# Transformer-block kernel on one Trainium2 core: two of v's seven products computed chunk by chunk beside the first norm, all of x loaded ahead, two combinations kept unsplit in DRAM, and the memory tokens ordered behind two state-space chunks

## The chip, the cores and the metric

The kernel runs on one core of a Trainium2 chip, as one program with one launch. The metric is device time in microseconds (us). A core has five engines that run their own instruction queues side by side: TensorE (PE in the profile; its weight loads are PEld), VectorE (DVE), ScalarE (ACT), GpSimd (POOL) and SyncE (SP), from whose queue this kernel issues all its DMAs.

## The reference, cut to what matters

One layer of a hybrid decoder trunk on x of 1024 tokens by 1024 channels, float32. The change touches the beginning of the first sub-layer, and the place where the second sub-layer's memory tokens are prepared.

```python
h = rms_norm(x, g_pre_mix[l])
q, k, v, z, xbc, dt_raw, ga, gs = _split(h @ w_in[l], IN_SIZES)
o_att = stick_breaking_attention(q..., k..., v...)      # 16 heads of 64
o_ssm = ssd_branch(z, xbc, dt_raw, conv_w[l], conv_b[l], dt_bias[l], a_log[l], d_skip[l], g_ssm_norm[l])
merged = jax.nn.sigmoid(ga) * (o_att @ w_br_att[l]) + jax.nn.sigmoid(gs) * (o_ssm @ w_br_ssm[l])
x = x + rms_norm(merged @ w_mix_out[l], g_post_mix[l])
h = rms_norm(x, g_pre_xa[l])
mem_n = rms_norm(mem, g_mem[l])                         # 256 memory tokens
x = x + rms_norm(memory_cross_attention(h, mem_n, w_xq[l], w_xkv[l], w_xo[l]), g_post_xa[l])
h = rms_norm(x, g_pre_ffn[l])
x = x + rms_norm(swiglu(h, w_gu[l], w_down[l]), g_post_ffn[l])
```

`h @ w_in` is one product of 1024 x 1024 with 1024 x 10272; v has 1024 of its columns, z 2048, dt 32.

## The kernel before, in words

**Split operands.** A float32 operand is rounded to the matmul's type as a high half (`hi_sb`, L85, a copy on ACT or POOL), and the rest becomes a low half (`lo_of`, L96, a subtraction on VectorE or POOL). A product of two operands is three matmuls: high by high, high by low, low by high (`mm3`, L99; `acc3`, L226, for four blocks of the inner dimension).

**Seven products in place of eight.** h transposed is cut into quarters: b11 and b21 are the two channel halves of tokens 0 to 511, b12 and b22 those of tokens 512 to 1023. Winograd's form of the 2 x 2 block product needs b11, b21, b22 and the combinations t1 = b12 - b11, t2 = b22 - t1, t3 = b22 - b12, t4 = b21 - t2, and on the weights a11, a21, a22, a12 the sums s1 = a21 + a22, s2 = s1 - a11, s3 = a11 - a21, s4 = a12 - s2. The seven products are a11 by b11, s2 by t2, a12 by b21, s1 by t1, s3 by t3, s4 by b22 and a22 by t4.

**First stage (L283 to L366).** x is loaded in chunks of 128 tokens (`load_x`, L293; four buffers of `t4`, so chunks 2, 6, 3 and 7 are loaded only when a buffer comes free). `chunk_pair(c)` (L319) takes chunks c and c + 4: `normed` (L305) squares on ACT (L309), makes the reciprocal root on POOL (L167, L168) and scales on VectorE (L310); `turned` (L313) does eight transposes per chunk on TensorE into PSUM; then come the splits of b11, b21 and b22 (L327, L328), the combinations on VectorE (L339 to L344) and their splits, those of t1, t3, t4 and b12 with the low half on POOL. The halves of b12 go to DRAM (`hb_d`) for the attention's projections. dt is made here with 48 small matmuls per pair (L354).

**v and z (L367 to L466).** `token_major(j, c0, put, i0)` (L392) runs the seven products of one block of 1024 columns: j = 0 is v, j = 1 and 2 are z. `product` (L400) splits four weight blocks and issues 48 matmuls of 128 x 512. The weight blocks come from DRAM into the ten buffers of `rp` ("zraw", L269). For v the sums s1, s2, s3 are made on VectorE (L424 to L428), for z on POOL. Then come the x, B, C columns and gates in `pair` (L523), dt's chain (`dt_chain`, L540), the attention, and the state-space mixer.

**State-space stage (from L839).** `prep(n)` (L916) loads the rows of chunk n and makes its decays (L930 to L939); two chunks are prepared ahead. `memory(m)` (L1058) loads and normalises 128 memory tokens; their key and value projections are spread over the first chunks (`mem_quanta`, L1072).

**What sets the order.** Every engine runs its queue in order. The order in a queue is not that of the code: a planner lays the instructions out before the launch, from modelled durations (`schedule_with_timeline_sim=True`, L1710), and a tile takes a buffer of its pool when one comes free. `behind(marks)` (L219) orders what it encloses behind given instructions on the same engine. `FILL_LEFT` and `FILL_RIGHT` (L31) are unused bytes that fix where later tiles lie.

## Time and profile before

| | |
|---|---|
| median of 3 runs | 2610.64 us (2610.59 to 2611.89) |
| the profiled execution | 2612.0 us |
| its span, first to last instruction | 2610.3 us |
| granted TensorE clock, mean | 0.984 |
| TensorE busy in the span | 2501.3 us (96%) |
| VectorE, ACT, POOL busy | 1801.2, 1142.9, 877.7 us |

Times in the profile are microseconds from the span's start. In a timeline row stand the start, the busy time, the engine, the line of the kernel, the operation, what it writes and reads, and the count; in brackets the idle time before it and what ended that. In a grouped row stand busy time, mean ns of one, and the idle time before. A row of the table by stretches has the stretch, its length, the busy time of PE, PEld, DVE, ACT and POOL with the instructions counted, the granted TensorE clock as a share of full speed, the busy share of the DMA engines and GB/s.

### The profile page before, as it was taken

The page shows a single profiled execution, that of the slowest core. Times are in us where ns is not written, and L with a number is a line of the kernel's source. Part 1 is how long each engine was busy: PE and PEld are TensorE (multiplying, and loading weights), DVE is VectorE, ACT ScalarE, POOL GpSimd, SP SyncE. Part 2 cuts the span into 40 slices and gives each one's busy share as a digit, 9 for nine tenths or more (in the row PEclk, how much of TensorE's full clock was granted, in tenths as well). Part 3 has the DMA queues.
Part 4 walks back from the last instruction along what each step waited for, and adds up shares of the span by engine and source line. Part 5 has one row for each costly group of instructions (what it writes and reads, how often), then busy time and mean ns, then how long its engine had stood idle before and what let it go on. Part 6 is the DMA issues. An engine that isn't in the chain of part 4 may idle for free. (4 is left out here: it accounts for less than half of the span.)

```text
span 2610.3 us, 32705 instructions
## 1 busy us (share of the span) xinstructions
PE 2501.3 (96%) x12026; PEld 2074.0 (79%) x12026; DVE 1801.2 (69%) x2084; ACT 1142.9 (44%) x2037; POOL 877.7 (34%) x682
## 2 busy tenths in 40 slices
PE   5999999999999999989999999999999999999997
PEld 5888887788878878878888778887787888887886
DVE  7446778776587887588888665415459666666996
ACT  5333454555465665456544312314324333333342
POOL 5212544453211112235555150101114333324763
PEclk7999999999999999989999999999999999999999
DMA  5331343333534343355332472311232232323223
GB/s 175 113 106 57 123 135 95 107 114 115 149 96 108 99 116 97 92 174 191 110 92 70 146 248 82 123 55 49 86 116 72 78 93 73 97 73 153 97 112 130
DMA packets 250667, 288.51 MB, mean 111 GB/s; under 512 B 16767, under 2 KB 173064, under 8 KB 250122
## 3 DMA queue, kind: packets, MB, share of 16 engines
q1 hardware_dynamic: 250506, 286.41, 35.1%
q8 instruction: 95, 1.56, 0.2%
q14 instruction: 66, 0.54, 0.1%
HBM read 196.56 MB, written 73.01 MB: 103 GB/s over the span
## 5 line engine op out<-in xcount | busy, mean ns | idle before, releaser
L750 DVE TENSOR_TENSOR_SCAN n<-n,mask 128x128 f32<-128x128 f32 (+7 forms) x128 | 188.8, 1500 | 23.5 <-ACT n L749 22.2
L97 DVE TENSOR_TENSOR sw<-sf,sw 128x512 fp32r<-128x512 f32 x150 | 127.1, 859 | 67.6 <-ACT sw L94 67.2
L198 POOL TENSOR_TENSOR sf<-wr,wr 128x512 f32<-128x512 f32 x38 | 57.5, 1514 | 275.1 <-DMA wr<-in_w_gu_dram 123.0
L767 ACT ACTIVATE wth<-tr,mone 128x512 fp32r<-128x512 f32 x192 | 110.4, 584 | 82.3 <-PE tr L764 81.6
L94 ACT ACTIVATE sw<-sf 128x512 fp32r<-128x512 f32 x150 | 92.0, 626 | 111.4 <-PE mm L231 96.0
L768 DVE SCALAR_TENSOR_TENSOR wtl<-tr,wth 128x512 fp32r<-128x512 f32 x192 | 99.7, 543 | 49.7 <-ACT wth L767 49.7
L94 ACT ACTIVATE sw<-wr 128x512 fp32r<-128x512 f32 x113 | 71.0, 629 | 127.6 <-PE mm L231 127.5
L231 PE MATMUL mm<-h,sw 128*128 128x512 f32 x320 | 124.8, 391 | 1.8 <-DVE sw L97 1.8
L100 PE MATMUL mm<-oth,bw 128*128 128x512 f32 (+1 forms) x320 | 122.4, 383 | 3.5 <-DVE a L1048 2.4
L229 PE MATMUL mm<-h,sw 128*128 128x512 f32 x320 | 122.8, 392 | 2.9 <-ACT h L94 2.3
L230 PE MATMUL mm<-h,sw 128*128 128x512 f32 x320 | 125.2, 391 | 0.0
L97 DVE TENSOR_TENSOR sw<-wr,sw 128x512 fp32r<-128x512 f32 x113 | 102.9, 911 | 26.0 <-ACT sw L94 18.0
L102 PE MATMUL mm<-oth,bw 128*128 128x512 f32 (+1 forms) x320 | 119.7, 374 | 0.0
L101 PE MATMUL mm<-otl,bw 128*128 128x512 f32 (+1 forms) x320 | 119.1, 372 | 0.0
L97 DVE TENSOR_TENSOR zl<-zr,zh 128x512 fp32r<-128x512 f32 x84 | 67.6, 810 | 72.4 <-ACT zh L94 72.3
L509 DVE SCALAR_TENSOR_TENSOR b<-b,prmT,b 128x1023 f32<-128x1023 f32 (+2 forms) x72 | 107.6, 1494 | 13.7 <-ACT b L507 13.1
L90 POOL TENSOR_SCALAR v<-va 128x512 fp32r<-128x512 f32 x16 | 20.5, 1286 | 284.8 <-PE av L777 164.8
L167 POOL TENSOR_SCALAR rstd<-ms 128x1 f32<-128x1 f32 x82 | 32.5, 396 | 238.0 <-ACT x L1269 112.0
L749 ACT ACTIVATE n<-sc 128x512 f32<-128x512 f32 (+1 forms) x192 | 88.6, 493 | 45.7 <-PE tr L764 28.9
L94 ACT ACTIVATE zh<-zr 128x512 fp32r<-128x512 f32 x84 | 52.4, 630 | 114.0 <-PE mb L415 55.4
L100 PE MATMUL p<-bw,h 128*128 128x512 f32 x256 | 98.9, 391 | 3.3 <-DVE x L1271 2.4
L200 POOL TENSOR_TENSOR sf<-wr 128x512 f32<-128x512 f32 x38 | 62.7, 1650 | 111.8 <-DVE sw L97 111.8
(596 smaller groups left out, 8247.3 us busy)
## 6 DMA issues: line engine op xcount, KB each, us to landing
wr<-in_w_gu_dram SPq DMA_DIRECT2D x80, 256.0 KB
wr<-in_w_in_dram SPq DMA_DIRECT2D x36, 512.0 KB
zr<-in_w_in_dram SPq DMA_DIRECT2D x24, 512.0 KB
gu_d<-t SPq DMA_DIRECT2D x44, 256.0 KB
wraw<-in_w_in_dram SPq DMA_DIRECT2D x20, 512.0 KB
x<-in_x_dram SPq DMA_DIRECT2D x16, 512.0 KB
zs_d<-zo SPq DMA_DIRECT2D x32, 256.0 KB
xs_d<-b SPq DMA_DIRECT2D x32, 256.0 KB
```

The costliest lines, as they stand in the source:

```text
L94: A.activation(o, i, AF.Copy)
L97: eng.tensor_tensor(o, i, hi.bitcast(F32), ALU.subtract)
L100: first = T.matmul(ps, sh, mh, start=start, stop=False)
L101: T.matmul(ps, sh, ml, start=False, stop=False)
L102: T.matmul(ps, sl, mh, start=False, stop=stop)
L229: T.matmul(ps, w[0][:, k, :], b[0][:, k, :], start=first and k == 0, stop=False, skip_group_check=True)
L230: T.matmul(ps, w[0][:, k, :], b[1][:, k, :], start=False, stop=False, skip_group_check=True)
L231: T.matmul(ps, w[1][:, k, :], b[0][:, k, :], start=False, stop=last and k == 3, skip_group_check=True)
L509: V.scalar_tensor_tensor(acc[:, sh:], y[:, :S - sh], cw(3 - sh, f), acc[:, sh:], ALU.mult, ALU.add)
L750: V.tensor_tensor_scan(nt[:, 0:L][:, ::-1], nt[:, 0:L][:, ::-1], mask[:, S - L:][:, ::-1], 1.0, ALU.mult, ALU.max)
L767: A.activation(wh[:, t0 * P:], pt[:, t0 * P:], AF.Identity, bias=mone)
L768: V.scalar_tensor_tensor(wl[:, t0 * P:], pt[:, t0 * P:], -1.0, wh[:, t0 * P:].bitcast(F32), ALU.add, ALU.subtract)
```

## The change

x0 is loaded first, then the gain and the other chunks, four of the eight into weight buffers, so that no load waits for a buffer. v's a11 and a12 are loaded in between and split once (`wv`). After each chunk pair, `first_products` runs the products of b11 and b21 for the chunk before, 24 matmuls of 128 x 512, keeps the first sum in `uv` and stores the first part of v. b12, t3 and t4 are stored unsplit (`hb_d`, `tc_d`); t3 and t4 are loaded and split in `rest_of_v`, which runs v's other five products, t1 first, with a11 and a12 loaded a second time; b12 is split when the attention needs it. dt takes high and low weights in one operand of 64 columns, 40 matmuls per pair in place of 48, and the two parts are added in `dt_chain`. The parameter columns and small loads move behind the last x; ACT gets a Square of one column at the very start; the transposes have five PSUM buffers in place of six. In the state-space stage the memory tokens' loads and first ACT work are ordered behind the loads and exponentials of the second chunk. z runs as before, with its sums on POOL.

```diff
-FILL_LEFT, FILL_RIGHT = 128, 224
+FILL_LEFT, FILL_RIGHT = 96, 224
...
-    dt_d = scr("dt_d", [32, S])
-    hb_d = [scr(f"hb_d{i}", [P, 4, HALF]) for i in range(2)]
+
+    dt_d = scr("dt_d", [2, 32, S])
+    hb_d = scr("hb_d", [P, 4, HALF])
+    tc_d = [scr(f"tc_d{i}", [P, 4, HALF]) for i in range(2)]
...
+    warm = mk(cp, [P, 1], F32, "warm")
+    A.activation(warm, mone, AF.Square)
...
-            bt = pool(p1, "b12t", 4)
+            bt = pool(p1, "b12t", 3)
+            vh = pool(p1, "vsplit", 8)
             mp = pool(p1, "memp")
             mt4 = pool(p1, "t4mem", 2)
             psp = pool(p1, "ps1", 2, PSUM)
+            xts = {}
+
+            def load_x(c):
+
+                xts[c] = mk(t4, [P, D], F32, "x4") if c % 4 >= 2 else mk(rp, [P, 2, HALF], F32, "zr").rearrange("p a t -> p (a t)")
+                return nc.sync.dma_start(xts[c], x_in[c * P:(c + 1) * P, :])
+
+            load_x(0)
             gx = load_gain(mp, "g_pre_mix")
-            xts = {}
-
-            def load_x(c):
-                xts[c] = mk(t4, [P, D], F32, "x4")
-                nc.sync.dma_start(xts[c], x_in[c * P:(c + 1) * P, :])
-
-            for c in (0, 4, 1, 5):
+            for c in (4, 1, 5):
                 load_x(c)
             wd = mk(mp, [P, KT, 32], F32, "wd")
             nc.sync.dma_start(wd, colblock(w_in, C_DT, 32))
-            wdh, wdl = [mk(mp, [P, KT, 32], F32R, n) for n in ("wdh", "wdl")]
-            hi_sb(wdh, wd, "p")
-            lo_of(wdl, wd, wdh, G)
+            raws = [block(0, C_V)]
+            for c in (2, 6):
+                load_x(c)
+            raws.append(block(512, C_V))
+            for c in (3, 7):
+                x_last = load_x(c)
+
+            def columns():
+
+                with behind([x_last]):
+                    nc.sync.dma_start(dsk, a["d_skip"][0].partition_broadcast(P))
+                    prm = [mk(mp, [P, P], F32, f"prm{i}") for i in range(2)]
+                    for t in prm:
+                        V.memset(t, 0.0)
+                    nc.sync.dma_start(prm[0][0:96, :], a["conv_w"][0].rearrange("t (f p) -> (t f) p", p=P))
+                    for nm, n in (("conv_b", 24), ("g_ssm_norm", 16)):
+                        nc.sync.dma_start(prm[1][rows[nm]:rows[nm] + n, :], a[nm][0].rearrange("(f p) -> f p", p=P))
+                pt = mk(psp, [P, 4, P], F32, "tr", bufs=5)
+                for i, t in enumerate(prm):
+                    T.transpose(pt[:, i, :], t, ident)
+                A.activation(prmT, pt[:, 0:2].rearrange("p i f -> p (i f)"), AF.Copy)
+
+            wds = mk(mp, [P, KT, 64], F32R, "wds")
+            hi_sb(wds[:, :, 0:32], wd, "p")
+            lo_of(wds[:, :, 32:64], wd, wds[:, :, 0:32], G)
 
...
-                pt = mk(psp, [P, 4, P], F32, "tr", bufs=6)
+                pt = mk(psp, [P, 4, P], F32, "tr", bufs=5)
...
-                q12 = [mk(bt, [P, 4, P], F32R, "b12") for _ in range(2)]
-                hi_sb(q12[0], t1, "a")
-                lo_of(q12[1], t1, q12[0], G)
-                for i in range(2):
-                    nc.sync.dma_start(hb_d[i][:, :, cs], q12[i].bitcast(F32))
-                V.tensor_tensor(t3, x22, t1, ALU.subtract)
-                V.tensor_tensor(t1, t1, x11, ALU.subtract)
+                y12 = mk(bt, [P, 4, P], F32, "b12")
+                A.activation(y12, x12, AF.Copy)
+                nc.sync.dma_start(hb_d[:, :, cs], y12)
+                V.tensor_tensor(t1, y12, x11, ALU.subtract)
+                V.tensor_tensor(t3, x22, y12, ALU.subtract)
+                nc.sync.dma_start(tc_d[0][:, :, cs], t3)
                 q22 = put("b22", x22)
                 V.tensor_tensor(t2, x22, t1, ALU.subtract)
                 q21 = put("b21", x21)
                 V.tensor_tensor(t4_, x21, t2, ALU.subtract)
+                nc.sync.dma_start(tc_d[1][:, :, cs], t4_)
                 put("t2", t2, V)
-                put("t1", t1, G)
-                put("t3", t3, G)
-                put("t4", t4_, G)
-                du = mk(mt4, [32, 2, P], F32, "du")
-                pdt = mk(psp, [P, HALF], F32, "pdt", bufs=2)
-                for i, q in enumerate(((q11, q21), (q12, q22))):
-                    for k in range(KT):
-                        hi, lo = q[k // 4]
-                        mm3(pdt[0:32, i * P:(i + 1) * P], wdh[:, k, :], wdl[:, k, :], hi[:, k % 4, :], lo[:, k % 4, :], k == 0, k == KT - 1)
-                A.activation(du, pdt[0:32, 0:2 * P].rearrange("h (i t) -> h i t", i=2), AF.Copy)
+                q1 = put("t1", t1, G)
+                du = mk(mt4, [64, 2, P], F32, "du")
+                pdt = mk(psp, [P, HALF], F32, "pdt", bufs=1)
+                for i, terms in enumerate((((0, q11), (4, q21)), ((0, q11), (4, q22), (0, q1)))):
+                    for n, (k0, q) in enumerate(terms):
+                        for k in range(4):
+                            for j in range(2):
+                                T.matmul(pdt[0:64, i * P:(i + 1) * P], wds[:, k0 + k, :], q[j][:, k, :],
+                                         start=n == k == j == 0, stop=n == len(terms) - 1 and k == 3 and j == 1)
+                A.activation(du, pdt[0:64, 0:2 * P].rearrange("h (i t) -> h i t", i=2), AF.Copy)
                 for i in range(2):
-                    nc.sync.dma_start(dt_d[:, (c + 4 * i) * P:(c + 4 * i + 1) * P], du[:, i, :])
-
-            raw0 = blocks(C_V)
+                    nc.sync.dma_start(dt_d[:, :, (c + 4 * i) * P:(c + 4 * i + 1) * P].rearrange("j h t -> (j h) t"), du[:, i, :])
+
+
+            wv = []
+            for raw in raws:
+                for k in range(4):
+                    w = raw[k // 2][:, k % 2, :]
+                    wv.append((mk(vh, [P, HALF], F32R, "vh"), mk(vh, [P, HALF], F32R, "vl")))
+                    hi_sb(wv[-1][0], w, "a")
+                    lo_of(wv[-1][1], w, wv[-1][0])
+            ut = [mk(rp, [P, 2, HALF], F32, "zr") for _ in range(2)]
+            uv = [ut[c // 2][:, c % 2, :] for c in range(4)]
+
+            def put_v(pl, tag, c, i, x):
+                vt = mk(pl, [P, HALF], F32, tag)
+                A.activation(vt, x, AF.Copy)
+                nc.sync.dma_start(v_d[1 + c * P:1 + (c + 1) * P, i * HALF:(i + 1) * HALF], vt)
+
+            def first_products(c):
+                cs = slice(c * P, (c + 1) * P)
+                ps = mk(psp, [P, HALF], F32, "pv")
+                for n, nm in enumerate(("b11", "b21")):
+                    acc3(ps, [t[:, :, cs] for t in hb[nm]], None, n == 0, n == 1, wv[4 * n:4 * n + 4])
+                    if n == 0:
+                        A.activation(uv[c], ps, AF.Copy)
+                put_v(bt, "b12", c, 0, ps)
+
             for c in range(4):
                 chunk_pair(c)
-                if c + 2 < 4:
-                    load_x(c + 2)
-                    load_x(c + 6)
-
-
+                if c == 0:
+                    columns()
+                else:
+                    first_products(c - 1)
+                if c == 1:
+                    with behind([x_last]):
+                        a21, a22 = block(0, C_V + HALF), block(512, C_V + HALF)
+            first_products(3)
+            a11, a12 = block(0, C_V), block(512, C_V)
+
+
+        hp3_ = pool(pa2, "hT3")
+        hb.update({n: tuple(mk(hp3_, [P, 4, HALF], F32R, n + s) for s in "hl") for n in HT[1:]})
         with ExitStack() as p1:
             kp = pool(p1, "zk", 9)
             op = pool(p1, "zo", 2)
...
                 V.tensor_tensor(sg, x, sg, ALU.mult)
                 nc.sync.dma_start(zs_d[c * P:(c + 1) * P, i * HALF:(i + 1) * HALF], sg)
 
-            def put_v(c, i, x):
-                vt = mk(op, [P, S], F32, "zo")[:, 0:HALF]
-                A.activation(vt, x, AF.Copy)
-                nc.sync.dma_start(v_d[1 + c * P:1 + (c + 1) * P, i * HALF:(i + 1) * HALF], vt)
...
+            def rest_of_v():
+
+                def bank(x):
+                    return [mk(psp, [P, HALF], F32, x) for _ in range(4)]
+
+                s1 = [mk(op, [P, S], F32, "zo").rearrange("p (k t) -> p k t", k=2) for _ in range(2)]
+                both(lambda q: V.tensor_tensor(s1[q], a21[q], a22[q], ALU.add))
+                pb_ = bank("mb")
+                product(pb_, s1, "t1", True, False, True)
+                both(lambda q: V.tensor_tensor(a21[q], a11[q], a21[q], ALU.subtract))
+                both(lambda q: V.tensor_tensor(a11[q], s1[q], a11[q], ALU.subtract))
+                pa_ = bank("ma")
+                product(pa_, a11, "t2", True, True)
+                both(lambda q: G.tensor_tensor(a12[q], a12[q], a11[q], ALU.subtract))
+                for nm, src in zip(HT[1:], tc_d):
+                    for k in range(4):
+                        t = mk(kp, [P, HALF], F32, "zk")
+                        nc.sync.dma_start(t, src[:, k, :])
+                        hi_sb(hb[nm][0][:, k, :], t, "a")
+                        lo_of(hb[nm][1][:, k, :], t, hb[nm][0][:, k, :])
+                w = []
+                for c in range(4):
+                    V.tensor_tensor(uv[c], uv[c], pa_[c], ALU.add)
+                    w.append(mk(kp, [P, HALF], F32, "zk"))
+                    V.tensor_tensor(w[c], uv[c], pb_[c], ALU.add)
+                product(pb_, a12, "b22", False, True)
+                pa_ = bank("ma")
+                product(pa_, a21, "t3", True, False)
+                for c in range(4):
+                    V.tensor_tensor(w[c], w[c], pa_[c], ALU.add)
+                    store_v(c + 4, 1, w[c])
+                product(pa_, a22, "t4", False, True)
+                for c in range(4):
+                    x = mk(kp, [P, HALF], F32, "zk")
+                    V.tensor_tensor(x, uv[c], pb_[c], ALU.add)
+                    store_v(c + 4, 0, x)
+                for c in range(4):
+                    x = mk(kp, [P, HALF], F32, "zk")
+                    V.tensor_tensor(x, uv[c], pa_[c], ALU.add)
+                    store_v(c, 1, x)
+
+            def store_v(c, i, x):
+                nc.sync.dma_start(v_d[1 + c * P:1 + (c + 1) * P, i * HALF:(i + 1) * HALF], x)
 
...
-                    nc.sync.dma_start(dtb[q * 32:(q + 1) * 32], a["dt_bias"][0].unsqueeze(1))
-                V.tensor_scalar(u, u, dtb, None, ALU.add)
+                    for t, src in zip((u, e), (dt_d[0], dt_d[1])):
+                        nc.sync.dma_start(t[q * 32:(q + 1) * 32], src[:, q * QT:(q + 1) * QT])
+                    with behind([x_last]):
+                        nc.sync.dma_start(dtb[q * 32:(q + 1) * 32], a["dt_bias"][0].unsqueeze(1))
+                V.scalar_tensor_tensor(u, u, dtb, e, ALU.add, ALU.add)
                 V.scalar_tensor_tensor(e, u, -1.0, u, ALU.mult, ALU.max)
...
-                nc.sync.dma_start(b12[i].bitcast(F32), hb_d[i])
+                raw = mk(rp, [P, 2, HALF], F32, "wr")
+                nc.sync.dma_start(raw, hb_d[:, 2 * i:2 * i + 2])
+                hi_sb(b12[0][:, 2 * i:2 * i + 2], raw, "a")
+                lo_of(b12[1][:, 2 * i:2 * i + 2], raw, b12[0][:, 2 * i:2 * i + 2])
...
+            d["issued"] = load, exps
...
-        for m in range(2):
-            memory(m)
+        with behind(chk[AHEAD - 1]["issued"]):
+            nc.sync.dma_start(gm, a["g_mem"][0].partition_broadcast(P))
+            for m in range(2):
+                memory(m)
```

More of the change, by code (lines that the diff above doesn't have):

```diff
@@ L541, in dt_chain @@
                 aneg = mk(cp, [P, 1], F32, "aneg")
[L542 to L543 removed]
+                with behind([x_last]):
+                    for q in range(4):
+                        nc.sync.dma_start(aneg[q * 32:(q + 1) * 32], a["a_log"][0].unsqueeze(1))
                 A.activation(aneg, aneg, AF.Exp)
```

88 lines of the change are left out of this document (33 added, 55 removed).

## Prediction

> **What bounds the kernel now.** I read the page first, then the table of busy time by stretches, then the stretches of the first 60 us one by one, and in these the timeline of each engine.
>
> ```profile
> PE 2501.3 (96%) x12026; PEld 2074.0 (79%) x12026; DVE 1801.2 (69%) x2084; ACT 1142.9 (44%) x2037; POOL 877.7 (34%) x682
> 0.00:56.70 56.70, 29.31 (x259) 25.94 (x259) 41.09 (x49) 32.07 (x60) 35.50 (x42) 0.81 0.60 201
> 56.70:136.10 79.40, 79.40 (x337) 65.45 (x338) 40.30 (x54) 29.67 (x50) 21.04 (x10) 0.96 0.30 94
> ```
>
> The columns after the stretch are busy PE, PEld, DVE, ACT, POOL, then granted clock, DMA share and GB/s. TensorE is the bound of the whole (96%), and from 56.7 on it never rests; before that it is busy for only 29.31 of 56.70 us, and there VectorE leads (41.09). So a microsecond is won by bringing TensorE's later work into that hole, or by ending the hole sooner.
>
> ```profile
> 3.01 1.97 SPq L295 DMA_DIRECT2D x<-in_x_dram  x4
> 8.70 1.28 ACT L309 ACT_TABLE_LOAD   x1 [8.70 <-DMA x<-in_x_dram]
> 12.14 1.28 DVE L310 SCALAR_TENSOR_TENSOR x<-x,rstd,g_pre_mix 128x1024 f32<-128x1024 f32 x1 [7.06 <-POOL rstd L168]
> 13.48 4.03 PE L316 MATMUL tr<-ident,x 128*128 128x128 f32 x16 [8.73 <-DVE x L310]
> 55.14 1.15 DVE L328 TENSOR_TENSOR t2l<-tc,t2h 128x512 fp32r<-128x512 f32 x1
> 56.69 2.07 PE L413 MATMUL ma<-zh,b11h 128*128 128x512 f32 x4 [0.98 <-ACT zh L94]
> 70.60 0.39 PE L413 MATMUL mb<-zh,t2h 128*128 128x512 f32 x1
> 81.48 0.39 PE L413 MATMUL ma<-zh,b21h 128*128 128x512 f32 x1
> 92.36 0.39 PE L413 MATMUL mb<-zh,t1h 128*128 128x512 f32 x1
> 135.88 0.39 PE L413 MATMUL mb<-zh,b11h 128*128 128x512 f32 x1
> ```
>
> The hole opens with a wait for the first x (8.70), then a table load, then VectorE works from 12.14 to 56.29 without a real pause. v's seven products follow: b11 56.69 to 70.60, t2 to 81.48, b21 to 92.36, and z begins at 135.88. A product at full clock is 92.36 - 81.48 = 10.88 us, 48 matmuls of 0.227; b11 took 13.91, 3.0 more, because it began at a low clock. All later work keeps its distance from 135.88, so the sum is made there.
>
> **The change part by part.** After it, five products (54.4 us) stand between the end of the last chunk's two products, which I call T, and the start of z. Today z starts at 135.88 = 81.48 + 54.4. The gain is 81.48 - T, less what is lost behind T.
>
> *Start.* x0 is issued first, at about 0.8 in place of 3.01 (2.2 us), ahead of the half-MB gain (1.3 us at the 396 GB/s quoted below), and the early Square takes the 1.28 us table load off the path: between 2.2 and 4.8 us; I take 4.5, as each piece is a row in series. First transposes then at 9.0, first normalised x at 7.6. The rest lands in time: 5.9 MB up to the second weight block, at 396 GB/s from about 3 us, is about 18 us, and the last x about 21.
>
> ```profile
> 10.00:20.00 10.00, 6.32 (x42) 5.58 (x43) 6.06 (x6) 7.77 (x14) 8.12 (x11) 1.00 1.07 396
> L310 DVE SCALAR_TENSOR_TENSOR x<-x,rstd,g_pre_mix 128x1024 f32<-128x1024 f32 x8 | 12.9, 1610 | 9.3 <-POOL rstd L168 9.3
> L328 POOL TENSOR_TENSOR t3l<-tc,t3h 128x512 fp32r<-128x512 f32 x4 | 5.4, 1344 | 4.7 <-DVE b21l L328 2.9 <-ACT t3h L327 1.8
> L424 DVE TENSOR_TENSOR zr<-zr,zr 128x1024 f32<-128x1024 f32 x2 | 2.9, 1474 | 0.0
> L426 DVE TENSOR_TENSOR zr<-zr,zr 128x1024 f32<-128x1024 f32 x2 | 3.5, 1751 | 0.0
> L428 DVE TENSOR_TENSOR zr<-zr,zr 128x1024 f32<-128x1024 f32 x2 | 2.4, 1222 | 0.0
> L439 DVE TENSOR_TENSOR zk<-zk,mb 128x512 f32<-128x512 f32 x4 | 2.6, 683 | 2.1 <-PE mb L415 2.1
> L97 DVE TENSOR_TENSOR zl<-zr,zh 128x512 fp32r<-128x512 f32 x33 | 27.5, 838 | 29.9 <-ACT zh L94 29.7
> L94 ACT ACTIVATE zh<-zr 128x512 fp32r<-128x512 f32 x33 | 20.5, 630 | 42.5 <-PE ma L415 20.5 <-PE mb L415 19.6 <-DVE zr L428 2.4
> ```
>
> *VectorE in the stage.* Out: the four weight sums of L424 and L426, 2.9 + 3.5 = 6.4 us. In: eight low halves of v's weights, 8 x 0.69 to 0.84 = 5.5 to 6.7. Per chunk its own eight subtractions and two norms stay. POOL loses three splits per chunk (b12, t3, t4), some 12 x 1.34 = 16 us; L310 took 1.28 alone and 1.61 on average, so up to 8 x 0.33 = 2.6 us of VectorE's time may go with them; I take 2. Its stretch of 44.2 becomes 44.2 - 6.4 + 6.1 - 2 = 42, that is 7.6 to about 50. The b11 and b21 operands of the last chunk come before its combinations, so VectorE is no longer what T waits for.
>
> *TensorE in the stage.*
>
> ```profile
> 17.72 1.46 PE L316 MATMUL tr<-ident,x 128*128 128x128 f32 x8
> 37.70 1.94 PE L316 MATMUL tr<-ident,x 128*128 128x128 f32 x8 [2.65 <-DVE x L310]
> 19.09 0.23 PE L102 MATMUL pdt<-b11h,wdl 128*32 128x128 f32 x1
> 20.41 0.22 PE L100 MATMUL pdt<-b,wdh 128*32 128x128 f32 x1
> 33.78 0.31 PE L102 MATMUL pdt<-b22h,wdl 128*32 128x128 f32 x1
> 34.74 0.31 PE L102 MATMUL pdt<-b22h,wdl 128*32 128x128 f32 x1
> 58.56 0.63 PE L414 MATMUL ma<-zl,b11h 128*128 128x512 f32 x1
> 58.99 0.63 PE L415 MATMUL ma<-zh,b11l 128*128 128x512 f32 x1
> ```
>
> At full clock: 64 transposes at 0.18 = 11.7; dt falls from 192 matmuls to 160 at (20.41 - 19.09) / 22 = 0.06 = 9.6 (64 weight columns in place of 32 do not change the moving length, so I keep the price; at the 128-column price of a transpose it would be up to 19 us more, which I think unlikely); 96 product matmuls at 0.227 = 21.8. Sum 43.1 from 9.0. To this come three estimates: 3 us of early idle (b21's weights are there only near 20), 3 us of low clock at the first products, as b11 shows above, and 4 us of waits between chunks, far below the 27.4 us (56.70 - 29.31) in which TensorE stands today, since products of the chunk before are ready to fill them. T = 9.0 + 43.1 + 10 = 62, and the gain 81.5 - 62 = 19.5. The ends: no waits at all gives 55; VectorE and TensorE in turn gives 72 (rivals). ACT's eight high halves of weights, four copies and four v stores, less twelve high halves, are four more of 0.63: about 35 of 50 us.
>
> *Behind T.* Product t1 needs two sums (1.22 each, as L428) and four splits, and their buffers lie, by my count of the pools, on the weights the last chunk still reads; the first two splits can be done under its last matmuls, the others under the first chunk's twelve: 1.5 us, between 0 and 5. VectorE then has 6 sums, 28 low halves and 20 additions, about 7.3 + 28 x 0.84 + 20 x 0.68 = 44 us beside 54.4 of TensorE: hidden, the t3 and t4 splits with more than 30 us to spare; uncovered, each costs 0.7. The second product waits for s2 behind the s1 sums and splits, about 11 us after the first sum begins, and t1 covers 10.9.
>
> ```profile
> 116.04 2.40 POOL L424 TENSOR_TENSOR zr<-zr,zr 128x1024 f32<-128x1024 f32 x1 [35.97 <-DVE zl L97]
> 118.53 2.73 POOL L426 TENSOR_TENSOR zr<-zr,zr 128x1024 f32<-128x1024 f32 x1
> 132.14 2.39 POOL L428 TENSOR_TENSOR zr<-zr,zr 128x1024 f32<-128x1024 f32 x1 [2.02 <-DVE zl L97]
> ```
>
> *z's sums.* Two of the ten weight buffers now hold the partial v until v ends. z's own sums, which POOL made from 116 on, 20 us ahead, can take a buffer only then: 2.40 + 2.73 + 2.40 + 2.73 + 2.39 = 12.7 us until the first half of s2, plus 0.63 for its split, against 10.9 us of b11. That is 2 us late (0 if the planner puts z's b21 product first, 5 if the clock falls too).
>
> *Costed at nothing.* The third quarter is now reloaded as one plain operand and split in the attention's first microseconds (2 x 1.06 on ACT, as the 128x1024 Square below, and 2 x 1.22 on VectorE); the products of the first two quarters run before it. dt's four more small loads hang under the pairs; uncovered, some 1.5 us. The parameter columns add two transposes and one copy to chunk 0, 1.4 us beside the first loads.
>
> ```profile
> 42.55 2.68 SPq L338 DMA_DIRECT2D hb_d<-b  x2
> ```
>
> On SP's queue twelve stores (b12, t3, t4 per chunk) stand in place of eight, and four of v; each waits there for its data, as this one for part of 2.68 us, and what stands behind, the second set of weights, is first wanted after T. The small loads (a_log, dt_bias, d_skip) move behind the last x and free the queue ahead of it.
>
> *Memory tokens.*
>
> ```profile
> 1105.00:1150.00 45.00, 34.29 (x161) 26.28 (x160) 40.33 (x52) 27.34 (x47) 15.62 (x16) 0.77 0.57 172
> 1113.62 0.35 SPq L1055 DMA_DIRECT2D bw<-in_g_mem_dram  x1
> 1120.15 1.06 ACT L1062 ACTIVATE bw<-wraw 128x1024 f32<-128x1024 f32 x1 [0.56 <-DMA wraw<-in_mem_dram]
> 1121.04 1.19 PE L937 MATMUL dec<-colrows,keyrows 128*128 128x512 f32 x2 [1.33 <-DMA colrows<-sum_d]
> ```
>
> Over 45 us here TensorE stands for 10.7. The gain and a token load (1 MB, 2.6 us at 396 GB/s) go out ahead of the rows that the first state-space chunk waits for (1.33 us), and a Square (1.06 + 0.19) stands ahead of its exponentials on ACT. Behind the change the chunk starts 1.3 to 3.5 us sooner, but the tokens' matmuls, which fill TensorE's gaps, come some 6 us later, and VectorE, busy for 40.33 of 45, has no less to do. I take 1.5 us of gain, between 3.5 and -3.
>
> **Sum.** 19.5 - 1.5 - 2 + 1.5 = 17.5 us. The profiled execution took 2612.0 (span 2610.3), 1.4 above the median of 2610.64: 2594.5 on its scale, 2593 on that of the median.
>
> **The rivals.** *TensorE nearly full:* the weights and x are all early and the planner fills every gap: T = 55, nothing lost behind it: 26.5 + 1.5 = 28 us, 2583. For it: only five transpose buffers and no data stand in the way. Against it: TensorE waits in order, and a chunk's chain crosses three engines.
>
> *VectorE and TensorE in turn:* the queue is in order; 24 product matmuls (5.4 us) sit ahead of the next chunk's transposes, and with five buffers in place of six VectorE waits for these. A chunk is then about 10 us of VectorE and 5.4 of products: 7.6 + 4 x 15.4 = 69, near 72 with the dt matmuls: gain 81.5 - 72 - 3.5 + 1.5 = 7.5, 2603.
>
> *Half clock, slower than before:*
>
> ```profile
> 40.00:45.00 5.00, 4.29 (x22) 3.93 (x23) 4.59 (x5) 3.51 (x7) 4.51 (x5) 0.50 0.17 52
> 45.00:50.00 5.00, 5.00 (x73) 5.00 (x72) 4.97 (x8) 2.98 (x7) 2.58 (x2) 0.92 0.20 57
> ```
>
> From 40 to 45 TensorE was busy for 4.29 of 5 us, nearly all transposes, and was granted 0.50; with the dt matmuls from 45 on 0.92, and 1.00 from 10 to 20 with both kinds mixed. If the stage stays at 0.50, the sum is 96 x 0.43 + 64 x 0.24 + 160 x 0.107 (0.96 / 9 above) = 74, T = 9 + 74 + 3 = 86: 4.5 us lost, 3.5 behind T, 1.5 regained: 2617. It turns to a loss once T passes 79.5, a mean clock of about 0.6 with TensorE always busy. Against it: products are ordinary matmuls, and under them the clock was 0.96 on average from 56.7 to 136.1. [...]
>
> *The gain is given back:* a later stage waits for something else (z's buffers, the tokens), and it comes out near 2609.
>
> **How the numbers follow.** Forecast (T from 57 to 67, 2588 to 2598) 0.52; nearly full 0.18; in turn 0.17; half clock 0.08; given back 0.05. The range 2584 to 2606 leaves out half clock, given back and the extreme of nearly full. A measurement of this kernel tells about 0.2%, 5.2 us, from no change: the first three cases are faster by more, except the tail of "in turn"; with that tail and the given-back case "same" gets 0.08, slower 0.08, faster 0.84.
>
> **What would show it.** The first z product (mb from b11h) should start near 120 in place of 135.88, the last chunk's products end near 62, the first normalised x near 7.6; the clock should be above 0.85 from 25 on. TensorE waits for x longer than 10 us in the stage would mean "in turn"; a clock near 0.5 with a full TensorE the last rival. A wait of z's t2 product for s2 should be near 2 us, and the first dec matmul should come 1 to 3 us nearer to the end of attention. I am wrong if VectorE runs past 56, or if the stages behind 140 are not simply shifted.

## The result, and the profile after

The changed kernel took 2617.72 us (median of 14 runs, 2615.6 to 2621.88), the kernel before 2610.93 beside it (14 runs): 1.0024 times, with a 95% interval of 1.0016 to 1.0032. A second set gave 1.0014 (1.0005 to 1.0022). By these ratios it is 4 to 6 us slower, where 17.5 us of gain were forecast. The profiled execution took 2618.15 us, with a span of 2616.4 (before: 2612.0 and 2610.3).

From the page of the changed kernel, its busy TensorE, and from its table by stretches the first stage, v's other five products, the begin of z, the last pair of the x/B/C columns, and the first 45 us of the state-space stage (columns as in the prediction):

```profile
PE 2506.4 (96%) x11994; PEld 2074.3 (79%) x11994; DVE 1809.3 (69%) x2092; ACT 1135.4 (43%) x2025; POOL 877.4 (34%) x670
```

```profile
0.00:59.30 59.30, 45.57 (x322) 38.63 (x322) 36.65 (x51) 33.31 (x63) 19.92 (x30) 0.97 0.78 261
59.30:118.50 59.20, 56.49 (x248) 46.41 (x249) 42.66 (x57) 19.79 (x33) 12.41 (x4) 1.00 0.48 151
118.50:140.00 21.50, 18.73 (x69) 14.45 (x68) 7.59 (x9) 6.70 (x12) 16.06 (x7) 0.84 0.13 41
650.00:663.00 13.00, 9.78 (x43) 7.77 (x41) 4.03 (x5) 5.71 (x8) 2.60 (x2) 0.87 0.55 166
1105.00:1150.00 45.00, 31.50 (x132) 23.61 (x132) 42.44 (x53) 26.96 (x48) 28.18 (x21) 0.74 0.50 150
```

The first two rows are the gain. TensorE is busy for 45.57 of the first 59.3 us, where it was busy for 29.31 of 56.7, at a clock of 0.97 in place of 0.81. The next three rows are where it goes: three stretches in which TensorE stands, and works at 0.74 to 0.87 after it has stood. Before the change z's begin had no wait. The end of the x/B/C columns stood some 6 us later, in this row of the kernel before:

```profile
656.00:669.00 13.00, 13.00 (x63) 10.66 (x63) 7.81 (x7) 5.11 (x8) 4.52 (x3) 0.97 0.45 136
```

In the state-space stage TensorE stood before too, but less: the row from 1105 to 1150 in the prediction has it busy for 34.29 of 45 us.

The same instructions in the timeline of the changed kernel, and then one of them in that of the kernel before:

```profile
6.84 1.28 DVE L319 SCALAR_TENSOR_TENSOR zr<-zr,rstd,g_pre_mix 128x1024 f32<-128x1024 f32 x1 [5.65 <-DMA g_pre_mix<-in_g_pre_mix_dram]
8.18 1.97 PE L325 MATMUL tr<-ident,zr 128*128 128x128 f32 x8 [8.18 <-DVE zr L319]
52.03 0.69 DVE L337 TENSOR_TENSOR t2l<-tc,t2h 128x512 fp32r<-128x512 f32 x1
58.85 0.39 PE L215 MATMUL pv<-vh,b21l 128*128 128x512 f32 x1
60.99 1.20 PE L444 MATMUL mb<-zh,t1h 128*128 128x512 f32 x4 [1.75 <-ACT zh L96]
63.20 0.50 PE L445 MATMUL mb<-zl,t1h 128*128 128x512 f32 x1 [1.02 <-DVE zl L99]
106.92 0.39 PE L444 MATMUL ma<-zh,t4h 128*128 128x512 f32 x1
130.57 2.07 PE L444 MATMUL ma<-zh,t2h 128*128 128x512 f32 x4 [2.64 <-ACT zh L96]
```

```profile
125.00 0.39 PE L413 MATMUL ma<-zh,t4h 128*128 128x512 f32 x1
```

The first x is normalised at 6.84, the last chunk's b21 product ends at 59.1 (58.85 plus one matmul at 0.23 us start to start), and v's t4 product begins at 106.92 in place of 125.00: 18.1 us of lead. I followed this lead through the trace: for one TensorE instruction at a time, its start after the change less its start before (minus is ahead). The table has all runs; the first column is v's t4 product, then z's t1 product, the t2 product of the first x/B/C pair, the first matmul of the attention stage, the first of the state-space stage, the first of the stage behind that, the first of the down projection, and the end of that projection's last matmul into `dnb`.

| run | v t4 (125.00) | z t1 (168.52) | first pair (301.51) | attention (668.24) | state-space (1113.42) | behind it (1498.35) | down (2369.91) | its end (2592.19) |
|---|---|---|---|---|---|---|---|---|
| changed | -18.1 | -12.7 | -11.1 | -6.2 | -7.8 | +2.6 | +2.8 | +6.4 |
| changed, again | -18.2 | -13.4 | -11.7 | -8.4 | -9.0 | +2.9 | -1.1 | +2.7 |
| tokens back | -16.5 | -11.0 | -9.4 | -5.0 | -6.8 | -7.0 | -9.1 | -7.5 |
| tokens alone | -1.1 | -1.1 | -1.2 | -2.5 | -3.5 | +0.6 | +0.7 | +1.9 |
| z sums by half | -16.4 | -16.3 | -14.6 | -16.4 | -16.5 | -10.5 | -13.0 | -12.7 |
| last pair | -18.1 | -13.1 | -11.5 | -9.5 | -9.6 | +1.4 | -3.3 | -0.7 |
| z sum, own buffers | -14.2 | -15.1 | -13.5 | -9.0 | -9.8 | -5.4 | -8.0 | -3.4 |
| tokens' loads early | -17.0 | -12.1 | -10.4 | -6.2 | -6.7 | -2.6 | -3.7 | -3.3 |
| three undone | -18.2 | -18.0 | -16.4 | -16.7 | -17.4 | -17.9 | -19.5 | -15.3 |

A row is to be read from left to right: where a number falls toward zero, that stage ran longer than before. "Tokens alone" is the kernel before up to the state-space stage and still stands 3.5 us ahead there: so much two executions of the same work can differ over 1100 us. The two profiles of the changed kernel agree within 1.6 us in every step but one: between "behind it" and "down" the first stays (+2.6 to +2.8) and the second gains 4.1 us (+2.9 to -1.1). So single steps under 2 us in the table prove nothing, and of that stage not even 4 us do. In its two profiles the changed kernel loses 4.8 to 5.4 us in z, 3.4 to 4.9 between the first pair and the attention, 10.4 to 11.9 in the state-space stage and 3.6 to 3.8 in the down projection. One step is not quite like for like: in every run with the new first stage, four of the 48 matmuls of z's b11 product stand ahead of v's t4 product (0.9 us of work), so the lead there is 0.9 us more than the first column says, and the loss in z too.

### The profile page after: what moved, and what is told of

It is laid out like the page before. It is cut to its first block, busy times and chain, and to the rows that moved or that the text cites. A ratio compares the mean times of both kernels' runs of the same rounds, so it can differ in the third digit from the quotient of the medians.

```text
span 2616.4 us, 32640 instructions
## 1 busy us (share of the span) xinstructions
PE 2506.4 (96%) x11994; PEld 2074.3 (79%) x11994; DVE 1809.3 (69%) x2092; ACT 1135.4 (43%) x2025; POOL 877.4 (34%) x670
## 5 line engine op out<-in xcount | busy, mean ns | idle before, releaser
L102 PE MATMUL mm<-oth,bw 128*128 128x512 f32 (+1 forms) x320 | 122.4, 383 | 3.6 <-DVE a L1134 2.9
L102 PE MATMUL p<-bw,h 128*128 128x512 f32 x256 | 98.9, 391 | 3.3 <-DVE x L1358 2.4
L104 PE MATMUL p<-bw,h 128*128 128x512 f32 x256 | 100.1, 392 | 0.0
L103 PE MATMUL p<-bw,h 128*128 128x512 f32 x256 | 99.8, 390 | 0.0
```

The costliest lines, as they stand in the source:

```text
L102: first = T.matmul(ps, sh, mh, start=start, stop=False)
L103: T.matmul(ps, sh, ml, start=False, stop=False)
L104: T.matmul(ps, sl, mh, start=False, stop=stop)
```

## The experiments

The first four ran beside one another on one chip, the others on a second one; each ratio is to the kernel before on the same chip, five rounds each. The changed kernel itself did not run beside the first four, so they are compared with both of its ratios, 1.0024 and, from the second chip, 1.0014.

**Tokens back.** The gain is issued, and the tokens prepared, where they stood before.

```diff
+        nc.sync.dma_start(gm, a["g_mem"][0].partition_broadcast(P))
...
-        with behind(chk[AHEAD - 1]["issued"]):
-            nc.sync.dma_start(gm, a["g_mem"][0].partition_broadcast(P))
-            for m in range(2):
-                memory(m)
+        for m in range(2):
+            memory(m)
```

> The changed kernel with one part undone: the memory tokens' gain and loads stand ahead of the state-space chunks again, as before the change. Theory: of the lead of about 17 us with which z begins, some 10 us are lost in the state-space stage because the tokens' transposes come too late to fill TensorE's gaps; undone, the time is near 2608 us, the tokens' first transposes start 8 us or more ahead of where they stand before the change, and the stage ends with a lead of 6 to 9 us. Rival: the lead is lost in that stage whatever the tokens do, because its order is planned anew and it waits for loads that do not move with it; then the time stays between 2615 and 2619.

Measured: 0.9983 (0.9975 to 0.9992), 2605.49 us. The stage loses nothing (-6.8 in, -7.0 out) where it lost 10.4, and the whole is 10.7 us better than 1.0024, 8.1 better than 1.0014. The theory holds for the size. Its detail about the tokens' transposes did not come true: the first ones start at 1120.05, 6.4 us ahead of where they stood before the change (1126.48) and not 8. Against the changed kernel (1124.38) they are 4.3 us sooner, and the second ones 10.1. The timeline of the stage in the changed kernel, and then in this one:

```profile
1105.58 1.10 PE L997 MATMUL dec<-cfm,bfm 128*128 128x128 f32 x8
1111.19 0.76 PE L1022 MATMUL dec<-colrows,keyrows 128*128 128x512 f32 x1
1124.38 1.09 PE L1152 MATMUL mm<-ident,wraw 128*128 128x128 f32 x8 [0.94 <-DVE wraw L1148]
1140.78 1.91 PE L1152 MATMUL mm<-ident,wraw 128*128 128x128 f32 x8
1147.90 1.12 PE L1097 MATMUL ptr<-ident,s 128*128 128x128 f32 x4 [3.93 <-ACT s L1084]
1150.09 0.41 PE L102 MATMUL mm<-oth,bw 128*128 128x256 f32 x1
```

```profile
1106.61 1.10 PE L997 MATMUL dec<-cfm,bfm 128*128 128x128 f32 x8
1115.42 1.19 PE L1022 MATMUL dec<-colrows,keyrows 128*128 128x512 f32 x2 [3.72 <-DMA colrows<-sum_d]
1120.05 1.91 PE L1153 MATMUL mm<-ident,wraw 128*128 128x128 f32 x8
1130.69 1.78 PE L1153 MATMUL mm<-ident,wraw 128*128 128x128 f32 x8
1137.87 0.39 PE L102 MATMUL mm<-oth,bw 128*128 128x256 f32 x1 [0.47 <-DVE otl L1156]
```

With the tokens held back, in the changed kernel, the first decay is made 5.6 us after the stage's start in place of 8.8 (7.6 before the change), as the change meant it, and the wait of 3.72 us for the rows is gone. But the tokens' own products (mm from bw and the tokens' halves) begin 44.5 us after the stage's start in place of 31.3. Until they begin, TensorE has little but the chunks, and a chunk's matmuls wait for its chain over the other engines. The longest of these waits in the changed kernel from 1105 to 1150 are two of `ptr` for ACT, which neither this run nor the kernel before has there (total, times, longest):

```profile
PE ptr L1097 <- ACT s L1084: 6.8, 2, 3.9
```

The table by stretches, the changed kernel first, shows the price:

```profile
1135.00:1140.00 5.00, 4.31 (x16) 3.48 (x16) 5.00 (x8) 1.90 (x3) 0.00 (x0) 0.50 0.37 107
1140.00:1145.00 5.00, 3.97 (x14) 2.85 (x12) 4.00 (x5) 1.52 (x4) 4.84 (x3) 0.59 0.23 56
1145.00:1150.00 5.00, 2.10 (x7) 1.91 (x8) 3.50 (x7) 2.88 (x7) 3.47 (x5) 0.75 0.17 52
```

```profile
1135.00:1140.00 5.00, 3.84 (x22) 2.80 (x23) 5.00 (x8) 2.40 (x5) 2.22 (x3) 1.00 0.63 169
1140.00:1145.00 5.00, 5.00 (x44) 5.00 (x43) 4.40 (x6) 0.95 (x3) 2.44 (x2) 1.00 0.41 123
1145.00:1150.00 5.00, 5.00 (x45) 5.00 (x45) 2.26 (x2) 3.72 (x8) 3.36 (x5) 1.00 0.60 187
```

In 15 us the changed kernel issues 37 matmuls at a clock of 0.50 to 0.75, the other 111 at 1.00. These are many small products, so the counts are no measure of work; the busy share and the clock are. Over the whole stage, with the same number of matmuls as before the change, TensorE stands for 22.3 us in place of 16.6 and is busy for 373.0 in place of 368.3: of the 10.4 us lost, 5.7 are waiting and 4.7 slower matmuls.

**Tokens alone.** The kernel before with this edit only.

```diff
-        nc.sync.dma_start(gm, a["g_mem"][0].partition_broadcast(P))
...
+            d["issued"] = load, exps
...
-        for m in range(2):
-            memory(m)
+        with behind(chk[AHEAD - 1]["issued"]):
+            nc.sync.dma_start(gm, a["g_mem"][0].partition_broadcast(P))
+            for m in range(2):
+                memory(m)
```

> The kernel before with the memory-token edit alone. Theory: it costs 8 to 10 us by itself, 2619 to 2621, with TensorE idle for more of the 45 us around the stage's first chunks and the tokens' matmuls 5 to 8 us later. Rival: the edit is harmless by itself (2609 to 2612) and the loss in that stage comes only together with the new first stage. The prediction had a gain of 1.5 us (2609).

Measured: 1.0018 (1.0008 to 1.0028), 4.7 us slower; the stage loses 4.0 us (-3.5 to +0.6). The edit costs time by itself and gains none, but half of what I expected. The planner wrote another order here than in the changed kernel: the tokens' first product begins 35.6 us after the stage's start, not 44.5.

**z's sums by half.** The order s1, s3, s2 is made for the first half of the channels and then for the second; a mark keeps the planner from sorting it back.

```diff
-                both(lambda q: E_.tensor_tensor(s1[q], a21[q], a22[q], ALU.add))
-                s3 = a21
-                both(lambda q: E_.tensor_tensor(s3[q], a11[q], a21[q], ALU.subtract))
-                s2 = a11
-                both(lambda q: E_.tensor_tensor(s2[q], s1[q], a11[q], ALU.subtract))
+                s3, s2 = a21, a11
+                for q in range(2):
+                    i = E_.tensor_tensor(s1[q], a21[q], a22[q], ALU.add)
+                    if q:
+                        issue_behind(i, mark)
+                    E_.tensor_tensor(s3[q], a11[q], a21[q], ALU.subtract)
+                    mark = E_.tensor_tensor(s2[q], s1[q], a11[q], ALU.subtract)
```

> The changed kernel, with the three sums of z's weights made half by half on GpSimd (sum, difference, sum of the first half, then of the second), so that the first half of the t2 product's weights is ready after 7 us of sums in place of 12. Theory: the wait of 2.6 us at z's t2 product and the low clock behind it go, 4 to 6 us of lead are kept at 300 us, and the time is 2612 to 2614 (the state-space stage is planned anew too, so the lead at 300 is the cleaner reading). Rival: t2 then waits for its second half, or for VectorE's low halves, as long as it did before: less than 1.5 us of lead kept, 2617 to 2619.

Measured: 0.9965 (0.9953 to 0.9977), 2599.75 us: 15 us better than 1.0024, three times what was expected (13 us better than 1.0014). GpSimd's timeline in the changed kernel (two halves to a row), then GpSimd and TensorE in this run:

```profile
118.09 4.74 POOL L503 TENSOR_TENSOR zr<-zr,zr 128x1024 f32<-128x1024 f32 x2 [39.85 <-DVE zk L486]
122.79 4.76 POOL L505 TENSOR_TENSOR zr<-zr,zr 128x1024 f32<-128x1024 f32 x2
127.50 4.67 POOL L507 TENSOR_TENSOR zr<-zr,zr 128x1024 f32<-128x1024 f32 x2
```

```profile
119.76 2.39 POOL L505 TENSOR_TENSOR zr<-zr,zr 128x1024 f32<-128x1024 f32 x1 [39.45 <-DVE zk L486]
122.23 2.39 POOL L508 TENSOR_TENSOR zr<-zr,zr 128x1024 f32<-128x1024 f32 x1
124.71 2.39 POOL L509 TENSOR_TENSOR zr<-zr,zr 128x1024 f32<-128x1024 f32 x1
```

```profile
135.78 1.19 PE L444 MATMUL ma<-zh,t2h 128*128 128x512 f32 x4 [0.71 <-ACT zh L96]
```

The first half of s2 is there at 127.1 in place of 129.8, and the wait of 2.64 us is one of 0.71. In the table z keeps its lead (-16.4 to -16.3), so about 5 of the 5.4 us are those of the sums. The rest is not: with this edit the planner also put the last transposes of the x/B/C stage behind the t4 product (nothing is lost there) and the tokens' first product 34.6 us after the state-space stage's start, and that stage loses 6.0 in place of 10.4. A total alone would have credited the sums with three causes.

**Last pair.** In `tail`, the last transposes of the x/B/C stage (`late`) are held behind the last matmul of the last t4 product (`t4_end`).

```diff
...
-                        T.transpose(pt[:, c * P:(c + 1) * P], acc[:, cc * P:(cc + 1) * P], ident)
+                        tr = T.transpose(pt[:, c * P:(c + 1) * P], acc[:, cc * P:(cc + 1) * P], ident)
+                        if late and c == 0:
+                            issue_behind(tr, t4_end[0])
```

> The changed kernel, with the last transposes of the x/B/C stage held behind the last pair's t4 product, where they stand before the change. Theory: the wait of 2.5 us for GpSimd's product and the low clock after it go, and about 4 us of lead are kept from there to the end: 2613 to 2615. Rival: the attention's first products then wait for the same data or for the third quarter's split, and nothing is kept: 2617 to 2619.

Measured: 1.0006 (0.9997 to 1.0014), 4.7 us better than 1.0024, 2.1 better than 1.0014. The place, in the changed kernel and in this run:

```profile
655.93 1.97 PE L578 MATMUL tr<-ident,b 128*128 128x128 f32 x8 [2.53 <-POOL b L590]
657.55 0.78 PE L213 MATMUL mm<-t4h,sw 128*128 128x512 f32 x1
```

```profile
655.03 0.50 PE L213 MATMUL mm<-t4h,sw 128*128 128x512 f32 x1 [0.78 <-DVE b L235]
657.89 1.03 PE L581 MATMUL tr<-ident,b 128*128 128x128 f32 x8
```

In the changed kernel the transposes wait 2.53 us for GpSimd, and the product behind them in the queue must wait with them; issued first, it waits 0.78 us, and the transposes behind it wait for nothing. From the last t3 matmul ahead of this place to the attention the lead stays at -9.5, where the changed kernel's went from -10.3 to -6.2, and in its second profile from -12.5 to -8.4: 4.1 us both times. The theory holds for this place.

**The changed kernel again.**

> The changed kernel once more, beside the other runs of this chip, so that they can be compared with it directly. Expected: 1.0024 times the kernel before, as measured first, with the losses of lead in the same places (z's second product, the last pair, the state-space stage); a loss that appears in one execution only, as the 3 us of the down projection may be, was chance.

Measured: 1.0014 (1.0005 to 1.0022). All four losses recur in the table, that of the down projection too (3.8 us). By the expectation that speaks against chance; the last section weighs it.

**z's first sum in buffers of its own.**

```diff
-                s1 = [mk(rp, [P, 2, HALF], F32, "zr") for _ in range(2)]
+                s1 = [mk(op, [P, S], F32, "zo")... if j == 1 else mk(rp, [P, 2, HALF], F32, "zr") for _ in range(2)]
```

> The changed kernel, with the first sum of z's first block of weights in two buffers of another pool, which are free since v's second product, so that it need not wait until v's last additions release the two that hold the partial v. The order and the engine of the sums stay. Theory: the buffers are the cause; GpSimd begins them some 10 us sooner, the wait at z's t2 goes, and 4 to 6 us of lead are kept at 250 us (the state-space stage is planned anew too and may give 3 to 4 us more: 2608 to 2613). Rival: the sums wait for the weights' transfers or for v's own last GpSimd work instead, and start at 118 as before: 2616 to 2619.

Measured: 0.9985 (0.9976 to 0.9994), 2606.57 us, 1.4 below the expected 2608 to 2613. From GpSimd's timeline in this run, the first s1 and the first s2:

```profile
95.09 2.39 POOL L503 TENSOR_TENSOR zo<-zr,zr 128x1024 f32<-128x1024 f32 x1 [13.80 <-ACT zh L96]
112.70 2.40 POOL L507 TENSOR_TENSOR zr<-zo,zr 128x1024 f32<-128x1024 f32 x1 [3.02 <-DVE zl L99]
```

The sums begin 23 us sooner (some 10 were expected), the first half of s2 is ready at 115.1, before z's b11 product goes on at 122.4, and TensorE has no wait from 118 to 142. So it was the two buffers of the partial v, and not GpSimd's speed or the weights' loads, that set when the sums begin.

**Tokens' loads early, their arithmetic late.**

```diff
-        with behind(chk[AHEAD - 1]["issued"]):
-            nc.sync.dma_start(gm, a["g_mem"][0].partition_broadcast(P))
-            for m in range(2):
-                memory(m)
+        nc.sync.dma_start(gm, a["g_mem"][0].partition_broadcast(P))
+        toks = [memory_load(m) for m in range(2)]
+        for n in range(AHEAD):
+            prep(n)
+        with behind(chk[AHEAD - 1]["issued"]):
+            for m in range(2):
+                memory(m, toks[m])
```

> The changed kernel with the gain and the tokens loaded ahead of the first rows, as before the change, while all their arithmetic stays behind the first two chunks. Theory: it is the place of the tokens' work in the engines' queues (VectorE is full from 1105 to 1140 and does the chunks first) that makes the token products late; the loads were not what they waited for: still 2615 to 2619, the first token product within 3 us of 1150. Rival: the loads behind the rows are late; then the first token product moves 5 us or more forward and half of the loss or more goes: 2608 to 2612.

Measured: 0.9995 (0.9984 to 1.0005), 2610.15 us, in the rival's range. The first token product comes 3.8 us sooner, 5.0 counted from the stage's start, between the two readings. From this run's timeline:

```profile
1106.72 1.74 PE L997 MATMUL dec<-cfm,bfm 128*128 128x128 f32 x8
1115.99 1.19 PE L1022 MATMUL dec<-colrows,keyrows 128*128 128x512 f32 x2 [4.13 <-DMA colrows<-sum_d]
1146.26 0.39 PE L102 MATMUL mm<-oth,bw 128*128 128x256 f32 x1 [0.87 <-DVE otl L1158]
```

The chunk waits for its rows again (4.13 us), its first decay comes 9.3 us after the stage's start and not 5.6, and yet the stage loses 4.1 us in place of 10.4. The tokens' first product stands 39.5 us behind the stage's start, between 31.3 and 44.5. So my theory, that only the place of the arithmetic counts, falls: the loads are 6.3 of the 10.4 us. And no run here gains by starting the chunks sooner; one that does this alone, with the tokens' products in their old place, is missing.

**Three undone.** The edits of "z's sums by half", "last pair" and "tokens back" together.

> The changed kernel with the three suspected losses taken away together: z's sums half by half, the last pair's transposes behind its t4 product, and the memory tokens ahead of the state-space chunks as before. Theory: the losses are separate, the 17.4 us of z's start reach the end less 1 to 2 us: 15 to 17 us faster than the kernel before, 2593 to 2595, and 23 us faster than the changed kernel. Rival: what one edit keeps the next stage gives back, because the planner orders the state-space stage anew each time: no faster than the run with the z sums alone (10 us faster than before, 2600).

Measured: 0.9946 (0.9934 to 0.9958), 2596.53 us: 14.1 us faster than the kernel before, and the fastest here. The lead stays between 16.4 and 19.5 us from v to the down projection; at z's t2 a wait of 0.75 us is left:

```profile
134.05 1.20 PE L447 MATMUL ma<-zh,t2h 128*128 128x512 f32 x4 [0.75 <-ACT zh L96]
```

It is 1.5 us above the expected 2593 to 2595, and 20 or 18 us faster than the changed kernel by its two ratios, where 23 were expected; 4.2 us are given back in the down projection. So the losses are separate, and the rival falls.

## Why the prediction was wrong, point by point

**What bounds the kernel, and the hole.** Right. The start (7.6 and 9.0 forecast, 6.84 and 8.18 measured), the end of VectorE's work (50; 52.7) and T (62; 59.1) were close: from 8.18 to T are 50.9 us, which is the 43.1 of work and 7.8 of idle time and low clock, where I had put 10. The dt matmuls with 64 weight columns start 0.06 us apart at full clock (20.99, 21.05, 21.11), the price that the sum kept. The clock of 0.97 rules out "half clock", and T "in turn" (72). That "half clock" named 2617, the time that was measured, is luck: nothing of its mechanism came.

**The clock in the first stage.** From 30 to 60, where each chunk's transposes and dt matmuls stand between products, the clock was granted at 1.00 (28.55 us busy of 30): here this order did not make the products begin slow. Slow were the dt matmuls from 14.3 to 16.9, 0.107 us apart, and the products from 24.4 to 25.7, 0.43 apart, behind a wait of 2.02 us for v's split weights (clock 0.50 from 24.5 to 27.5). (The first clock record of the trace is at 17.66, that of the kernel before at 18.53; the rows count the time before it as full clock, so the 1.00 from 10 to 20 that the prediction names was hardly a reading of the clock.)

**Behind T.** 1.5 us forecast; the waits are 1.75 + 1.02 = 2.8, and with the slower matmuls around them 3.4 are lost. T was 2.9 us earlier than forecast. The lead of 18.1 us (19.0 with the four z matmuls) against the forecast 18.0 is two errors that nearly cancel.

**z's sums.** The mechanism was right (the two buffers of the partial v), and the term was mis-sized: 2 us forecast, 5.4 lost by the table, 6.2 with the four z matmuls counted. The wait was 2.64 us, but behind it TensorE ran its matmuls at 0.63 us busy in place of 0.39 for about 6 us (clock 0.50 from 130.57 to 137), which cost another 3.4. I had this as an end of the range ("5 if the clock falls too") and did not take it into the sum.

**Memory tokens: the step that failed.** The prediction has "I take 1.5 us of gain, between 3.5 and -3". It is a loss of 10.4 and 11.9 us in the two profiles, outside both ends. I saw that the tokens' matmuls fill TensorE's gaps and would come "some 6 us later"; relative to the stage's start they came 13.4 us later (44.5 less 31.1; before, 1144.55 less 1113.42). The chunk's first decay did come 2.0 us nearer to the stage's start, as forecast, and I priced that as if it ended the stage. Over all runs the loss goes with this delay, in groups (the run at 39.5 loses no more than those near 35). The delay was not varied with all else in place, since the planner orders the stage anew each time; what is shown is that the token edit costs it, and that the loss follows the delay roughly:

| run | first token product after the stage's start | the stage's loss |
|---|---|---|
| before; tokens back; three undone | 31.1; 31.3; 30.9 | 0; -0.2; -0.5 |
| z sums by half; z sum, own buffers; tokens alone | 34.6; 35.2; 35.6 | 6.0; 4.4; 4.0 |
| tokens' loads early | 39.5 | 4.1 |
| changed; again; last pair | 44.5; 44.7; 44.7 | 10.4; 11.9; 11.0 |

**"The stages behind 140 are simply shifted."** They are not, and I had named this as what would prove me wrong without giving it a price. The last pair lost 4.1 us, because the planner set its last two groups of eight transposes one product earlier than before, the second of them ahead of t4. The first pair lost 1.6 us in every run with the new first stage: its first matmuls wait 1.18 + 1.47 us for split weights from GpSimd, where they waited 0.38 + 0.74 before; why these come later was not tried. The down projection lost 3.6 and 3.8.

**The rivals.** "Given back" was the one that came, with a chance of 0.05 and a price near 2609: it named both places, z's buffers and the tokens, and had them end at no gain. That these two and three further places (first pair, last pair, down projection) add up to 24 us (18.1 ahead to 6.4 behind) was in none of the cases; "slower" with 0.08 rested on the clock alone.

Taken together, 5.4 + 1.6 + 4.9 - 1.6 + 10.4 + 0.2 + 3.6 = 24.5 us lost between v and the end in the profile of the changed kernel; three of these terms are undone in the last run, which keeps 14.1 of the 17.5 us forecast.

## What to carry to other kernels

A stage that hands a lead to later stages keeps it only if nothing in them is set by a buffer, a load or a written order that does not move with it, so give each later hand-over a price of its own, including the clock after its wait (here 3.4 us behind z's wait of 2.64). Work that fills the bound engine's gaps should be prepared early even at the cost of the chain beside it: here no run gained by a chain that starts 3 us sooner, and filler that came 13 us later went with a loss of 10. Where a planner writes the order, an edit changes orders far behind it, so judge each experiment by the lead at several places and not by its total.

## What the runs showed of the hardware that was not expected

The clock fell behind short waits, and not behind each of them. In the changed kernel it was 0.50 from 24.5 to 27.5, behind a wait of 2.02 us that ended at 24.36; from 130.57 to 137, behind the wait of 2.64 us at z's t2; and from 656 to 659, behind the wait of 2.53 us in the last pair. At v's t1 product the waits were 1.75 and 1.02 us both in the changed kernel and in the run "z sum, own buffers", with the same order of work, and the clock from 65 to 70 was 1.00 in the first and 0.50 in the second:

```profile
65.00:70.00 5.00, 5.00 (x24) 4.12 (x23) 5.00 (x7) 2.95 (x7) 3.24 (x1) 1.00 0.90 251
```

```profile
65.00:70.00 5.00, 5.00 (x13) 3.84 (x12) 5.00 (x8) 2.30 (x4) 2.15 (x1) 0.50 0.76 227
```

In these 5 us 24 matmuls began, or 13. Of the 3.9 us by which that run's first column (-14.2) stands below the changed kernel's, 2.8 are this clock; the other 1.1 were lost before the t1 product began (62.09 in place of 60.99). So here the length of the waits alone did not tell the clock behind them; what did, no run shows.

The down projection runs the same order of TensorE instructions in every kernel, and its length still varied by up to 4.6 us (from the last two columns: 0.3 in "z sums by half", 4.6 in "z sum, own buffers"). Its waits are much alike; the clock behind them is not. The changed kernel, then "z sums by half", from 37.3 us after the projection's start in both:

```profile
2410.00:2420.00 10.00, 7.40 (x27) 5.02 (x26) 10.00 (x11) 2.75 (x3) 8.49 (x6) 0.86 0.00 0
2420.00:2430.00 10.00, 10.00 (x37) 8.01 (x37) 8.92 (x11) 3.70 (x7) 7.02 (x4) 0.80 0.01 2
```

```profile
2394.17:2404.17 10.00, 6.91 (x28) 4.59 (x27) 10.00 (x12) 2.55 (x3) 7.78 (x5) 1.00 0.00 0
2404.17:2414.17 10.00, 10.00 (x45) 7.90 (x44) 8.91 (x11) 4.19 (x7) 7.04 (x4) 1.00 0.01 2
```

From 2350 to 2600, in five of the profiles, TensorE's idle time ahead of its matmuls into `dna` and `dnb` adds up to 5.7 to 6.3 us. The 324 matmuls into `dna` from `op` took 402 to 408 ns on average, by line, in the changed kernel and 403 to 405 in "three undone", which lost 3.6 and 4.2 us in the projection; in the kernel before, "z sums by half" and "tokens' loads early" they took 391 to 399, and at most 0.4 us was lost. So in these the loss is slower matmuls more than longer waits. By the last two columns of the table five profiles lost 2.6 to 4.6 us in the projection (the changed kernel twice, "last pair", "z sum, own buffers", "three undone"), the other five 0 to 1.6. The loss goes with no single edit, so I take it for luck of the single execution, although both profiles of the changed kernel had it; that is not shown, and no experiment was aimed at it.
